# The key's norm in a stick-breaking attention: applied to the keys, or to the logits when they are evicted

## Chip, core and metric

One core of a Trainium2 chip runs the whole program. The metric is the device time of one execution in microseconds.

## What is computed

A two-layer decoder trunk over 1024 tokens of width 1024: a gated DeltaNet layer with its feed-forward part, then a cross layer whose eight heads (128 wide) attend by stick-breaking over keys and values computed once. The part that matters here, cut from the reference:

```python
def rms_norm(x, gain):
    y = x * lax.rsqrt(jnp.mean(x * x, axis=-1, keepdims=True) + EPS)
    return y * gain

k = rms_norm(k.reshape(b_, s_, SB_HEADS, SB_DH), k_gain)      # per token and head
q = rms_norm((hn @ w_q).reshape(b_, s_, SB_HEADS, SB_DH), q_gain)

z = jnp.einsum('bhtd,bhsd->bhts', qb, kb) * scale             # 128 queries, all keys up to them
ls_neg = jax.nn.log_sigmoid(-z)
log_fail = jnp.where(causal, ls_neg, 0.0)
log_rest = lax.cumsum(log_fail, axis=3, reverse=True) - log_fail
att = jnp.where(causal, jnp.exp(z + ls_neg + log_rest), 0.0)
outs.append(jnp.einsum('bhts,bhsd->bhtd', att, vb))
```

The norm of a key is one number per token s, so it may multiply the key's 128 elements, or column s of the logits.

## The kernel before

Matrix products run on pairs of fp32r tiles, a rounded part `h` and the remainder `l`, as three matmuls (h.h, h.l, l.h) into one PSUM buffer. PSUM has two sets: `ups`, three buffers, for projections; `ips`, five buffers, for transposes, logits and attention times values. A buffer is given to the next user when its last reader is done. In SBUF the tag `n` has four buffers of 128x1024, shared in this stage by the copies of projections (`f` of k, q and v), the attention's output `of`, the two parts `nh`/`nl` of one row of output weights, and, at the end, rows of the residual stream.

The stage around the change is written as generators whose steps carry a cost. `sb_steps(hd)` (attention of head `hd`) and `qkv_steps(hd + 1)` (k, q and v projections of the next head) are merged in the ratio of ATT 24000 to QKV 35000; for the last head the second stream is `part(fill, BESIDE)`, the first output projections (`down_steps`, L257 to L259, whose results ScalarE copies out at L308). This gives the order in which the program is written down; a scheduler that assigns buffers and semaphores may move an instruction ahead of others on its engine when it reckons it ready, and the order on each engine is then fixed in the program.

A projection is done in two halves of 512 tokens, 24 matmuls each (L140 to L142), with head dimension on partitions and tokens along the free axis. What is done with a half at its end is its `take`; steps that come later are put on a list by `post(delay, ...)` and run when the clock of the projection stream has passed their time.

- Query: `take` copies the half to `f` (L1516) and evicts `ql`, `qh` with the gain from the projection's buffer (L1517, L1518). 3000 later, `norm` transposes `f` (L1488, four 128x128 blocks into one `ips` buffer), squares (L1493, ScalarE), sums (L1494, VectorE) and takes the power -1/2 (L1495, L1496, GpSimd). The result has queries on partitions, and is the scale `sc` of the logits' eviction.
- Key: `take` only copies (L1550). `norm` as above, then `scale` (2000 later) multiplies the transposed block, still in its PSUM buffer, by the norm back into `f` (L1538, VectorE), and `back` (3000 later) transposes `f` again (L1488) and evicts `kh` (L1545, ScalarE) and `kl` (L1546, VectorE) with the gain.
- Value: `take` copies (L1568); 3000 later `rows` transposes and evicts `vh`, `vl` (L1563, L1564).

For each block of 128 queries, `sb_logs` makes up to two logit tiles of up to 512 keys (L1590 to L1592), from each of which ScalarE takes Abs with scale (L1593) into `l` and VectorE the scaled logit into `z` (L1594); then ScalarE does Exp (L1598) and Ln (L1599) on `l`. `sb_weights`, one block later: VectorE max and add (L1607), GpSimd's causal selects (L1609), VectorE's scan (L1613) and subtraction (L1614), ScalarE's Exp (L1616). Another block later, `sb_transpose` transposes the weights (L1629) and evicts them (L1631 ScalarE, L1632 VectorE); `sb_values` multiplies by the values (L1646 to L1648), copies out (L1650) and stores the head (L1656). Weight columns come in by DMA (L112), are scaled on GpSimd (L121) and split (L103 ScalarE, L104 VectorE).

Of the kernel before, what the change touches and what calls it, by code (L numbers as in the profile page):

```python
# [12 lines left out]
AF = mybir.ActivationFunctionType  # L13
ALU = mybir.AluOpType
# [4 lines left out]
P = 128  # L19
# [4 lines left out]
def yoco_kernel(  # L24
# [22 lines left out]
    act, dve, pool, pe, sp = nc.scalar, nc.vector, nc.gpsimd, nc.tensor, nc.sync  # L47
# [10 lines left out]
    HB = S // 2  # L58
# [16 lines left out]
    def i_tile(shape=(P, 4, P)):  # L75
        return pi.tile(list(shape), F32, tag="i", name="ips")

    def n_tile(shape=(P, S)):
        return main.tile(list(shape), F32, tag="n", name="n", bufs=4)
# [4 lines left out]
    def bc(ap, n=P):  # L84
        return ap.unsqueeze(2).broadcast_to([ap.shape[0], ap.shape[1], n])


    ident = cpool.tile([P, P], F32, name="ident")
# [82 lines left out]
    def run(gen):  # L171
        for _ in gen:
            pass
# [803 lines left out]
    with tc.tile_pool(name="gdn", bufs=1) as gp:  # L977
# [50 lines left out]
        def gain_cols(i, j, n):  # L1028
            return gains[:, offs[i] + j * n : offs[i] + (j + 1) * n]
# [4 lines left out]
        g_k = gain_cols(4, 0, 1)  # L1034
# [423 lines left out]
    with tc.tile_pool(name="sba", bufs=1) as ap_:  # L1458
        tc.keep_in_program_order(act.preload_act_table_set("natural_log_exp_and_others"))

        def sb_tile(tag, nm):
            return ap_.tile([P, S], F32R, tag=tag, name=nm, bufs=4 if tag != "v" else 3)

        posts, clock = [], [0]
        POST, SCALE, BACK = 3000, 2000, 3000

        def post(delay, fn, *args):
            posts.append((clock[0] + delay, fn, args))
            posts.sort(key=lambda p: p[0])
# [15 lines left out]
        def transpose_half(f, hf):  # L1485
            tps = i_tile()
            for j in range(4):
                pe.transpose(tps[:, j, :], f[:, hf * HB + j * P : hf * HB + (j + 1) * P], ident)  # L1488
            return tps

        def row_norm(s_, tps):
            sq = main.tile([P, 4, P], F32, tag="og", name="sq")
            act.activation(sq, tps, AF.Square, scale=float(P) ** -0.5)  # L1493
            dve.tensor_reduce(s_, sq, axis=AX.X, op=ALU.add)  # L1494
            pool.tensor_scalar(s_, s_, EPS, None, op0=ALU.add)  # L1495
            pool.tensor_tensor(s_, s_, mhalf, op=ALU.pow)  # L1496

        def z_tile(tag):
            return ap_.tile([P, S], F32, tag=tag, name=tag, bufs=3 if tag == "z" else 2)

        def f_tile(hd):
            return z_tile("z") if hd == 0 else n_tile()
# [19 lines left out]
            return take  # L1522

        def k_take(hd):
            f = f_tile(hd)
            hi, lo = sb_tile("k", "kh"), sb_tile("k", "kl")
            qkv[hd, "k"] = (hi, lo)

            def norm(hf):
                tps = transpose_half(f, hf)  # L1530
                ss = ap_.tile([P, 4], F32, tag="ss", name="ss", bufs=4)
                row_norm(ss, tps)
                post(SCALE, scale, hf, tps, ss)
                return 436

            def scale(hf, tps, ss):
                fs = f[:, hf * HB : (hf + 1) * HB].rearrange("p (a b) -> p a b", b=P)
                dve.tensor_tensor(fs, tps, bc(ss), op=ALU.mult)  # L1538
                post(BACK, back, hf)
                return 1  # L1540

            def back(hf):
                hs = slice(hf * HB, (hf + 1) * HB)
                tf = transpose_half(f, hf).rearrange("p a b -> p (a b)")
                act.activation(hi[:, hs], tf, AF.Copy, scale=g_k)  # L1545
                dve.scalar_tensor_tensor(lo[:, hs], tf, g_k, hi[:, hs], op0=ALU.mult, op1=ALU.subtract)  # L1546
                return 436

            def take(hf, sl, ps):
                act.copy(f[:, sl], ps)  # L1550
                post(POST, norm, hf)

            return take
# [19 lines left out]
        qkv, zs, ats, ofs = {}, {}, {}, {}  # L1573
# [3 lines left out]

        def sb_logs(hd, tb, later):

            (qh, ql, qs), (kh, kl) = qkv[hd, "q"], qkv[hd, "k"]  # L1580
            w = (tb + 1) * P
            ts_ = slice(tb * P, (tb + 1) * P)
            z, l = z_tile("z"), z_tile("l")
            sc = qs[:, tb : tb + 1]
            next(later, None)
            for s0 in range(0, w, 512):
                n = min(512, w - s0)
                ss_ = slice(s0, s0 + n)
                zps = i_tile((P, 512))
                pe.matmul(zps[:, :n], qh[:, ts_], kh[:, ss_], start=True, stop=False)  # L1590
                pe.matmul(zps[:, :n], qh[:, ts_], kl[:, ss_], start=False, stop=False)
                pe.matmul(zps[:, :n], ql[:, ts_], kh[:, ss_], start=False, stop=True)  # L1592
                act.activation(l[:, ss_], zps[:, :n], AF.Abs, scale=sc)  # L1593
                dve.tensor_scalar(z[:, ss_], zps[:, :n], sc, None, op0=ALU.mult)  # L1594
                yield 3 * max(107, n * 0.417)
                next(later, None)
            run(later)
            act.activation(l[:, :w], l[:, :w], AF.Exp, scale=-1.0)  # L1598
            act.activation(l[:, :w], l[:, :w], AF.Ln, bias=1.0)  # L1599
            chains[hd, tb] = (z, l)  # L1600
# [57 lines left out]
        def sb_order():  # L1658

            blocks = [(hd, tb) for hd in range(H) for tb in range(NT)]  # L1660
            n = len(blocks)
            for k in range(n + 3):
                at_ = blocks[min(k, n - 1)][0]
                later = sb_weights(*blocks[k - 1]) if 1 <= k < n + 1 else iter(())
                yield at_, sb_logs(*blocks[k], later) if k < n else later
                if 2 <= k < n + 2:
                    yield at_, sb_transpose(*blocks[k - 2])
                if k >= 3 and blocks[k - 3][1] % 2:
                    hd, tb = blocks[k - 3]
                    yield at_, sb_values(hd, tb // 2)  # L1670
# [14 lines left out]
        def head_all(hd):  # L1685
            takes = [k_take, q_take, v_take]
            if hd == 0:
                yield from proj_two_steps(norm1, [(la1.ready.pop(0), takes.pop(0)(hd)) for _ in range(2)])
                la1.fill(2)
            for take in takes:  # L1690
                last = hd == H - 1 and take is takes[-1]
                for i, cost in enumerate(proj_steps(xT, la1.get(), take(hd))):
                    yield cost
                    if last and i in (1, KT + 1):
                        next(fill)
# [92 lines left out]
```

## Time and profile before

| | us |
|---|---|
| median of 3 runs (2637.34 to 2642.93) | 2642.91 |
| the profiled execution | 2642.97 |
| its span | 2641.3 |
| TensorE busy | 2540.1 (96%) |
| VectorE busy | 1829.7 (69%) |
| ScalarE busy | 1144.9 (43%) |
| GpSimd busy | 863.8 (33%) |

The stage of the change fills about 1405 to 1910 us of the span. TensorE's busy time has the modelled ends of pipelined matmuls in it: neighbours overlap, so that gaps between them show a little smaller than they are. An instruction's row in the timeline gives start, duration, engine, line, and in brackets how long the engine stood idle before it and what released it.

### The profile page before, as it was taken

What the parts mean: (1) busy time and instruction counts of PE and PEld (TensorE: products, weight loads), DVE (VectorE), ACT (ScalarE), POOL (GpSimd) and SP (SyncE); (2) the same over time, 40 slices, a digit from 0 to 9 for tenths busy, and PEclk for the clock granted to TensorE, in tenths of its full rate; (3) what the DMA queues carried; (4) which work ended last, traced back from release to release, by engine and by line L of the source; (5) the groups of instructions that cost most, each with busy time, mean ns of one, the idle gap of its engine ahead of it and who ended that gap; (6) DMA issues with size and microseconds to landing.
All of it is one profiled execution on the core that took longest, in us unless ns stands there. A gap on an engine that the chain in (4) does not pass through costs nothing.

```text
span 2641.3 us, 35798 instructions
## 1 busy us (share of the span) xinstructions
PE 2540.1 (96%) x12908; PEld 2068.3 (78%) x12908; DVE 1829.7 (69%) x2705; ACT 1144.9 (43%) x2219; POOL 863.8 (33%) x1262
## 2 busy tenths in 40 slices
PE   8999999999999999998999999999999999999999
PEld 6777877887768888886777778887777888887777
DVE  6667766775686666667755778877658566666774
ACT  6333333334363444432215667667646444443220
POOL 2444444444411222254313243333240212225420
PEclk9999999999999999999999999999999999999999
DMA  4221222223324554578661111111333455548765
GB/s 125 63 58 54 65 54 65 69 72 100 132 65 143 170 145 134 165 248 296 230 221 66 39 34 33 32 41 63 105 128 88 122 158 168 144 136 288 272 224 203
DMA packets 368953, 331.25 MB, mean 125 GB/s; under 512 B 19572, under 2 KB 321791, under 8 KB 368775
## 3 DMA queue, kind: packets, MB, share of 16 engines
q1 hardware_dynamic: 368774, 328.96, 39.9%
q8 instruction: 101, 1.65, 0.3%
q14 instruction: 78, 0.63, 0.1%
HBM read 226.10 MB, written 102.79 MB: 125 GB/s over the span
## 4 chain that ended last, share of the span: by engine, by line
PE 58%; DVE 14%; issue 12%; POOL 5%; ACT 5%; DMA 4%; SPq 0%; POOLq 0%; DVEq 0%; ACTq 0%
PE ips L453 6%; PE ips L454 6%; PE ips L455 6%; PE ups L140 5%; PE ups L454 4%; PE ups L455 4%; PE ups L453 4%; PE ups L141 4%; PE ups L142 4%; DVE l L1613 2%; PE ips L1143 2%; DVE wl L104 2%; PE ups L258 2%; PE ups L259 2%; PE ups L257 2%
## 5 line engine op out<-in xcount | busy, mean ns | idle before, releaser
L140 PE MATMUL ups<-x,wh 128*128 128x512 f32 (+1 forms) x912 | 388.7, 427 | 0.0
L142 PE MATMUL ups<-x,wl 128*128 128x512 f32 (+1 forms) x912 | 363.1, 399 | 0.0
L141 PE MATMUL ups<-x,wh 128*128 128x512 f32 (+1 forms) x912 | 359.4, 394 | 0.0
L453 PE MATMUL ips<-x,w 128*128 128x512 f32 x840 | 328.5, 393 | 7.3 <-ACT x L359 3.7
L454 PE MATMUL ips<-x,w 128*128 128x512 f32 x840 | 328.7, 391 | 2.7 <-DVE x L360 2.7
L455 PE MATMUL ips<-x,w 128*128 128x512 f32 x840 | 327.5, 390 | 0.0
L552 POOL TENSOR_TENSOR n<-n,ev 128x512 f32<-128x512 f32 x44 | 70.2, 1596 | 627.4 <-ACT n L551 627.4
L453 PE MATMUL ups<-x,w 128*128 128x512 f32 x648 | 252.0, 392 | 2.0 <-ACT x L359 2.0
L454 PE MATMUL ups<-x,w 128*128 128x512 f32 x648 | 253.5, 391 | 0.3 <-DVE x L360 0.3
L455 PE MATMUL ups<-x,w 128*128 128x512 f32 x648 | 252.7, 390 | 0.0
L142 PEld LDWEIGHTS ups<-x,wl 128*128 128x128 f32 (+1 forms) x912 | 170.8, 187 | 37.4
L453 PEld LDWEIGHTS ips<-x,w 128*128 128x128 f32 x840 | 157.6, 188 | 46.6 <-ACT x L359 6.3
L140 PEld LDWEIGHTS ups<-x,wh 128*128 128x128 f32 (+1 forms) x912 | 171.9, 189 | 22.6 <-ACT x L231 0.2
L141 PEld LDWEIGHTS ups<-x,wh 128*128 128x128 f32 (+1 forms) x912 | 172.2, 189 | 21.4 <-DVE x L232 0.2
L454 PEld LDWEIGHTS ips<-x,w 128*128 128x128 f32 x840 | 158.0, 188 | 39.0 <-DVE x L360 5.8
L455 PEld LDWEIGHTS ips<-x,w 128*128 128x128 f32 x840 | 157.9, 188 | 32.7
L746 DVE TENSOR_TENSOR h<-h,ips 128x512 f32<-128x512 f32 x176 | 119.4, 682 | 61.5 <-PE ips L455 61.3
L453 PEld LDWEIGHTS ups<-x,w 128*128 128x128 f32 x648 | 121.5, 188 | 28.9 <-ACT x L359 3.6
L454 PEld LDWEIGHTS ups<-x,w 128*128 128x128 f32 x648 | 121.9, 188 | 26.8 <-DVE x L360 1.6
L455 PEld LDWEIGHTS ups<-x,w 128*128 128x128 f32 x648 | 121.9, 188 | 24.9
L746 DVE TENSOR_TENSOR h<-h,ups 128x512 f32<-128x512 f32 x136 | 92.5, 682 | 47.0 <-PE ups L455 46.7
L104 DVE TENSOR_TENSOR wl<-raw,wh 128x1024 fp32r<-128x1024 f32 x65 | 83.5, 1284 | 53.9 <-ACT wh L103 51.4
(377 smaller groups left out, 5983.4 us busy)
## 6 DMA issues: line engine op xcount, KB each, us to landing
raw<-in_ffn_w_gu_dram SPq DMA_DIRECT2D x88, 512.0 KB, 4.8
w<-hsa SPq DMA_DIRECT2D x88, 512.0 KB, 4.6
hsa<-w SPq DMA_DIRECT2D x116, 256.0 KB, 3.1
hb<-hsb SPq DMA_DIRECT2D x68, 384.0 KB, 4.2
raw<-in_ffn_w_down_dram SPq DMA_DIRECT2D x44, 512.0 KB, 4.3
raw<-in_gdn_w_in_dram SPq DMA_DIRECT2D x32, 512.0 KB, 4.2
hsb<-w SPq DMA_DIRECT2D x54, 256.0 KB, 3.6
hsa<-n SPq DMA_DIRECT2D x48, 256.0 KB, 3.6
```

Source lines behind the costliest of these rows:

```text
L104: dve.tensor_tensor(lo, raw, hi, op=ALU.subtract)
L140: pe.matmul(o, wh[:, kt, :m], xh, start=kt == 0, stop=False)
L141: pe.matmul(o, wh[:, kt, :m], xl, start=False, stop=False)
L142: pe.matmul(o, wl[:, kt, :m], xh, start=False, stop=kt == KT - 1)
L257: pe.matmul(ps, ah[:, sl], wh[:, ns], start=i == 0, stop=False)
L258: pe.matmul(ps, ah[:, sl], wl[:, ns], start=False, stop=False)
L259: pe.matmul(ps, al[:, sl], wh[:, ns], start=False, stop=i == n - 1)
L453: pe.matmul(ps, ah, bh, start=start, stop=False, skip_group_check=True)
L454: pe.matmul(ps, ah, bl, start=False, stop=False, skip_group_check=True)
L455: pe.matmul(ps, al, bh, start=False, stop=stop, skip_group_check=True)
L552: pool.tensor_tensor(s, s, self.t3, op=ALU.mult)
L746: dve.tensor_tensor(d, d, ps, op=ALU.add)
```

## The change

The keys are no longer scaled. `kh` and `kl` are evicted in `take`, unscaled by the norm, from the projection's buffer, as the query's are. `norm` computes the four columns of a half (128 tokens on partitions, 4 blocks). `scale` and `back` are gone; 6000 after `norm`, `spread` transposes each column, repeated 128 times along the free axis, which gives 128 equal rows with tokens along the free axis, and ScalarE copies the four blocks to `rk`: 128x1024, the key's norm of each token on all partitions. `rk` is the key's own `f` (for head 0 a new `n` tile) and lives until the logits of its head are done. The logits' eviction multiplies by `sc` and by `rk` on VectorE; Abs then reads `z` from SBUF instead of the logits from PSUM.

```diff
-        POST, SCALE, BACK = 3000, 2000, 3000
+        POST, SPREAD = 3000, 6000
...
         def k_take(hd):
+
+            hi, lo = sb_tile("k", "kh"), sb_tile("k", "kl")
             f = f_tile(hd)
-            hi, lo = sb_tile("k", "kh"), sb_tile("k", "kl")
-            qkv[hd, "k"] = (hi, lo)
+            rk = [None if hd == 0 else f]
+            qkv[hd, "k"] = (hi, lo, rk)
 
             def norm(hf):
-                tps = transpose_half(f, hf)
                 ss = ap_.tile([P, 4], F32, tag="ss", name="ss", bufs=4)
-                row_norm(ss, tps)
-                post(SCALE, scale, hf, tps, ss)
+                row_norm(ss, transpose_half(f, hf))
+                post(SPREAD, spread, hf, ss)
                 return 436
 
-            def scale(hf, tps, ss):
-                fs = f[:, hf * HB : (hf + 1) * HB].rearrange("p (a b) -> p a b", b=P)
-                dve.tensor_tensor(fs, tps, bc(ss), op=ALU.mult)
-                post(BACK, back, hf)
-                return 1
-
-            def back(hf):
-                hs = slice(hf * HB, (hf + 1) * HB)
-                tf = transpose_half(f, hf).rearrange("p a b -> p (a b)")
-                act.activation(hi[:, hs], tf, AF.Copy, scale=g_k)
-                dve.scalar_tensor_tensor(lo[:, hs], tf, g_k, hi[:, hs], op0=ALU.mult, op1=ALU.subtract)
+            def spread(hf, ss):
+                if rk[0] is None:
+                    rk[0] = n_tile()
+                bps = i_tile()
+                for j in range(4):
+                    pe.transpose(bps[:, j, :], ss[:, j : j + 1].broadcast_to([P, P]), ident)
+                act.copy(rk[0][:, hf * HB : (hf + 1) * HB], bps.rearrange("p a b -> p (a b)"))
                 return 436
 
             def take(hf, sl, ps):
                 act.copy(f[:, sl], ps)
+                act.activation(hi[:, sl], ps, AF.Copy, scale=g_k)
+                dve.scalar_tensor_tensor(lo[:, sl], ps, g_k, hi[:, sl], op0=ALU.mult, op1=ALU.subtract)
                 post(POST, norm, hf)
...
-            (qh, ql, qs), (kh, kl) = qkv[hd, "q"], qkv[hd, "k"]
+            (qh, ql, qs), (kh, kl, (rk,)) = qkv[hd, "q"], qkv[hd, "k"]
...
-                act.activation(l[:, ss_], zps[:, :n], AF.Abs, scale=sc)
-                dve.tensor_scalar(z[:, ss_], zps[:, :n], sc, None, op0=ALU.mult)
+                dve.scalar_tensor_tensor(z[:, ss_], zps[:, :n], sc, rk[:, ss_], op0=ALU.mult, op1=ALU.mult)
+                act.activation(l[:, ss_], z[:, ss_], AF.Abs)
```

## Rows read from the trace of the kernel before

**Rows 1.** The page, engines: busy us (share of the span) x instructions.
```profile
PE 2540.1 (96%) x12908; PEld 2068.3 (78%) x12908; DVE 1829.7 (69%) x2705; ACT 1144.9 (43%) x2219; POOL 863.8 (33%) x1262
```

**Rows 2.** Windows: length, busy us per engine (instructions), granted clock, DMA share, GB/s.
```profile
1440.00:1840.00 400.00, 380.18 (x2099) 320.37 (x2098) 318.60 (x440) 269.06 (x495) 142.43 (x236) 1.00 0.12 38
1840.00:1910.00 70.00, 61.57 (x316) 50.99 (x315) 43.62 (x61) 46.02 (x85) 18.55 (x24) 0.95 0.34 112
```

**Rows 3.** TensorE's waits, 1440 to 1840: us in total, times, longest.
```profile
PE ips L1488 <- DVE z L1594: 7.5, 10, 2.2
PE ips L1590 <- DVE kl L1546: 6.3, 6, 1.2
PE ips L1629 <- ACT z L1616: 2.5, 4, 0.9
PE ips L1488 <- DVE n L1538: 1.6, 1, 1.6
```

**Rows 4.** Timeline around a wait for `kl`: start, us, engine, line, operation, [idle before].
```profile
1578.09 0.62 PE L1488 MATMUL ips<-ident,n 128*128 128x128 f32 x4
...
1578.77 0.58 ACT L1493 ACTIVATE sq<-ips 128x512 f32<-128x512 f32 x1
...
1582.77 0.72 DVE L1546 SCALAR_TENSOR_TENSOR kl<-ips,gains,kh 128x512 fp32r<-128x512 f32 x1
...
1583.54 0.50 PE L1590 MATMUL ips<-kh,qh 128*128 128x512 f32 x1 [1.23 <-DVE kl L1546]
...
1583.88 0.39 PE L1591 MATMUL ips<-kl,qh 128*128 128x512 f32 x1
...
1584.11 0.40 PE L1592 MATMUL ips<-kh,ql 128*128 128x512 f32 x1
...
1585.20 0.68 DVE L1538 TENSOR_TENSOR n<-ips,ss 128x512 f32<-128x512 f32 x1
```

**Rows 5.** Timeline at the boundary of two heads.
```profile
1610.54 1.06 ACT L1616 ACTIVATE z<-z 128x1024 f32<-128x1024 f32 x1 [4.93 <-DVE z L1614]
...
1613.71 0.34 DVE L1594 TENSOR_SCALAR z<-ips,ssq 128x128 f32<-128x128 f32 x1
...
1614.11 0.65 PE L1488 MATMUL ips<-ident,n 128*128 128x128 f32 x4 [1.42 <-DVE z L1594]
```

**Rows 6.** Groups by form, 1400 to 1915: count | busy us, mean ns | idle before.
```profile
L1594 DVE TENSOR_SCALAR z<-ips,ssq 128x512 f32<-128x512 f32 x48 | 35.7, 743 | 4.4 <-ACT l L1593 4.4
L1593 ACT ACTIVATE l<-ips,ssq 128x512 f32<-128x512 f32 x48 | 33.0, 688 | 6.2 <-PE ips L1592 6.0
...
L1488 PEld LDWEIGHTS ips<-ident,n 128*128 128x128 f32 x232 | 26.4, 141 | 16.0 <-DVE z L1594 9.6 <-ACT n L1568 2.1 <-issue 2.0
...
L1538 DVE TENSOR_TENSOR n<-ips,ss 128x512 f32<-128x512 f32 x14 | 9.6, 684 | 9.6 <-POOL ss L1496 9.6
...
L1598 ACT ACTIVATE l<-l 128x512 f32<-128x512 f32 x8 | 5.2, 644 | 0.0
```

**Rows 7.** Timeline at the end of head 6, and line L308, 1840 to 1900.
```profile
1829.20 0.74 DVE L1594 TENSOR_SCALAR z<-ips,ssq 128x512 f32<-128x512 f32 x1
...
1830.31 0.60 PE L1488 MATMUL ips<-ident,n 128*128 128x128 f32 x4
...
1831.66 1.21 DVE L104 TENSOR_TENSOR nl<-raw,nh 128x1024 fp32r<-128x1024 f32 x1
...
1833.80 0.61 ACT L1568 COPY n<-ups 128x512 f32<-128x512 f32 x1
...
1842.19 0.66 PE L1488 MATMUL ips<-ident,n 128*128 128x128 f32 x4 [1.48 <-ACT n L1568]
...
1870.05 0.32 SPq L1656 DMA_DIRECT2D oT<-n  x1
...
L308 ACT COPY x<-ups x16: 567/587/635, 1849.5 to 1895.9; 128x512 f32<-128x512 f32 x16
```

**Rows 8.** Timeline, the last transposes that waited for the exponential before 1840.
```profile
1461.09 0.66 PE L1629 MATMUL ips<-ident,z 128*128 128x128 f32 x4 [0.85 <-ACT z L1616]
```

## Prediction

> **What bounds the kernel now.** The page's engine shares come first: TensorE is busy 96% of the span [rows 1], so time is gained only where TensorE stands still or runs slowly. The change touches one stage, the stick-breaking attention, so next I read the windows of that stage. From 1440 to 1840 us, while the attention of heads 0 to 6 runs beside the projections of heads 1 to 7, TensorE is busy 380.18 of 400 us, VectorE 318.60, ScalarE 269.06; from 1840 to 1910, head 7 beside the first output projection, TensorE has 61.57 of 70 us and a granted clock of 0.95 [rows 2]. What can be won in the first window is thus 19.8 us of visible gaps, plus some 0.16 us a gap (a 512-column matmul is drawn 0.39 long but the next starts 0.23 after it [rows 4]). Then TensorE's waits: the largest are transposes waiting for the logits' eviction on L1594 (7.5 us), the first logit matmul waiting for `kl` on L1546 (6.3 us), attention transposes waiting for the exponential L1616 (2.5 us), and one wait of 1.6 us for the key scaling L1538 [rows 3]. None of the first two is a data dependence: the transposes don't read `z`, and that matmul reads an older head's keys. They wait for a PSUM buffer: `ips` has five, and all transposes, logits and values take turns in them.
>
> The timeline around one such wait shows why. The norm's transposes of a key half start at 1578.09; their square has read them by 1579.35, yet the buffer is held until L1538 has read it too, at 1585.88, because that instruction waits for the GpSimd power. The buffer of the way back is held until L1546 ends at 1583.49, and TensorE's matmul starts at 1583.54, after 1.23 us of nothing [rows 4]. This wait comes five times at 1.23 us and once at 0.15 (6.3 us in six) [rows 3].
>
> **The change part by part.**
> 1. *L1538 goes.* Sixteen halves, 0.684 us each [rows 6]: 10.9 us of VectorE, which isn't the bound. Its worth is the buffer: the norm's is now free after the square (0.58 us [rows 4]) instead of 6.5 us later.
> 2. *`kh` and `kl` are made at the take, from the projection's own PSUM buffer `ups`*, as the query does it. L1545/L1546 move (0.72 us for the latter [rows 4]), at no cost. They hold `ups` longer; there are three, a projection half takes 24 matmuls at 0.23 = 5.5 us, and that covers it. Without the cover, each half would cost the 0.7 us of one eviction. The way back's hold of `ips` until L1546 is gone.
> 3. *`spread` is added*: four transposes replace the four of the way back, one for one, and one ScalarE copy of 128x512 per half: as the output projection's copy of the same shape, 0.587 [rows 7], 16 of them 9.4 us, beside TensorE. It is due 9000 cost units after the take where the way back was due 8000; `rk` is read a head later, so the 1000 cost nothing. ScalarE is busy 67% in the window [rows 2] and hides it; uncovered on the way to the buffer it costs 0.6 a half. The copy frees its `ips` buffer; it stands where `kl` stood but doesn't wait behind VectorE's scans. The stationary operand is one column read 128 times, which no row shows. The nearest row is the ordinary fp32 weight load at 0.141 us [rows 6]; I take that. Bounds: half and double of it, 64 loads x 0.07, from -4.5 to +4.5 us when none is hidden by a running matmul (as an estimate from that row).
> 4. *The logits' eviction.* Before, ScalarE's Abs reads the buffer (0.688 us), then VectorE (0.743) [rows 6], one after the other. Now VectorE alone reads it, with `rk` as second tensor: the nearest row with a PSUM input and a second SBUF tensor is L1546 at 0.72 [rows 4], so at par with 0.743. The Abs then reads `z` from SBUF; nearest row, the SBUF-to-SBUF L1598 at 0.644 against 0.688 [rows 6]: 48 x 0.044 = 2 us less on ScalarE. So each logit buffer can be free some 0.7 us earlier, and VectorE needn't wait for ScalarE to free it. The price is latency: z, Abs, Exp, Ln now stand in one row where Abs came first and z ran beside Exp, +0.70 us per block; and Abs now sits in ScalarE's queue until VectorE has done z, with the takes' copies and the attention casts behind it.
>  [...]
> 5. *`rk` lives in an `n` buffer* (four of them, shared by the takes' copies, the attention's output `of`, and two weight tiles `nh`, `nl`) until the last logits of its head. Between heads this just fits. At the end of head 6 it doesn't: `rk` of head 6 is read until 1829.9 (L1594), `rk` of head 7 and `of` of head 6 stay (its last store is issued at 1870.05), the query's copy until its transposes at 1830.31. `nh` and `nl` (now at 1831.66) take the two that come free, and the value's copy, now at 1833.80, finds none until `of` is stored [rows 7]. Two of three `ups` buffers stay full, and the output projection beside it runs on one: each of its steps waits for its own copy. Sixteen copies run from 1849.5 to 1895.9, one per 3.1 us [rows 7]; in the 28 us from 1842 to 1870 that is nine steps x 0.587 = 5.3 us at most, less what attention work fills. Lower bound 0 (head 7's attention moves up instead and frees `of` early). If the value's copy gets its buffer first, `nl` waits for the transposes at 1842.19 [rows 7], 2 to 3 us late. I take 3 us.
>
> *Sum, against the profiled execution (span 2641.3, time 2642.97, as good as the median 2642.91).*
> - `kl` waits gone: 5 x (1.23 + 0.16) + 0.3 = 7.3 us, all.
> - L1538's wait gone: 1.6 + 0.16 = 1.8.
> - The waits on L1594: ten, 7.5 us, the longest 2.2 [rows 3]; the long ones lie at the head boundaries. There ScalarE stands 4.93 us for the last block's L1614, the weight cast and VectorE's L104 behind it come late, and the 128-column z is only evicted at 1613.71, whereupon the transposes start at 1614.11 [rows 5]. With z no longer behind Abs it may go before L104, and it may not, since the order on VectorE is set when the kernel is built. Half: 0.5 x (7.5 + 10 x 0.16) = 4.6.
> - Against it: head 0's four waits for L1616 (2.5 us in four [rows 3], at the stage's start, where blocks are short) grow by up to 0.70 each; half, 1.4. Tail: 3.
>
> 7.3 + 1.8 + 4.6 - 1.4 - 3.0 = 9.3 us gained: 2642.97 - 9.3, about **2634 us**. Next late behind the removed waits are the attention transposes behind `attl` and L1616.
>
> **The rivals.**
> - *Gaps come back.* With `ips` free earlier TensorE runs into the next buffer or into L1616, whose own chain VectorE's scans set; VectorE is 80% busy [rows 2]. For it: VectorE loses only 3% of its work. Against: the five 1.23 us waits have two buffers of five returned, not one. Half of the `kl` gain and none of the boundary's remain: 3.7 + 1.8 + 1 - 1.4 - 3 = 2 us, **2641**.
> - *The longer row sets the end (slower).* Place: ScalarE's queue at Abs. If ScalarE, waiting for z behind a scan, delays casts by more than TensorE's reserve of other matmuls, each block pays the 0.70 us. It decides from the point where L1616 is waited for in steady state; today the last of its four waits ends at 1461.09 [rows 8]. At 64 blocks x 0.70 = 45 us in full; at half of heads 0 and 7 and a fifth of the others (8 + 48 x 0.2 = 18 blocks, 12 us) against 2 us of gain left: **2653**. [...]
> - *The `n` buffers bite harder (slower).* If the store of `of` or `nl` comes so late that the output projection stops altogether from 1842 to 1870, nine steps x 9 matmuls x 0.23 = 18.6 us move out of cover; half is refilled later by the attention: -12.3 of gain + 9.3, **2640**, and in full **2649**.
> - *It doesn't do what it says*: the transposes of a repeated column cost double (+4.5) and the freed buffers are hidden anyway: **2645**.
>
> **How the numbers follow.** Forecast (2626 to 2638) 0.56; gaps come back 0.22; longer row 0.10; buffers 0.08 (half of it on each side of the bound); not as said 0.04. The low end takes all listed waits (7.3 + 1.8 + 9.1), no tail cost and half of the transposes' bound (2.2): 20.4 us, 2622. The high end reaches to 2650, short of the full longer row. The bound of 0.2% is 5.3 us (about what a measurement of this kernel can tell from no change): below 2637.6 faster, above 2648.2 slower. Faster: the forecast and a little of the second case, 0.58; same 0.27; slower 0.15.
>
> **What would show it.** Right: no wait of L1590 for the keys' eviction; the norm's transposes freed by the square; ScalarE's Abs released by VectorE's z, VectorE's z by TensorE; TensorE idle from 1440 to 1840 down from 19.8 to some 8 us; the value's copy of head 7 late, near the last store of `of`, and the steps of L257 slowed there. Wrong: waits of L1629 for L1616 in heads 1 to 6, weight loads of the spread above 0.19 us, or a window to 1910 longer than 470 us.

## The result, and the profile after

The changed kernel is slower: 2675.31 us, the median of four runs (2671.61 to 2677.34), against 2642.66 for the kernel before on the same chip. The ratio is 1.0122, with a 95% interval of 1.011 to 1.0134; in time 32 us lost, where 9 us gained were forecast. The profiled execution took 2677.34 us, its span is 2675.4.

The page of the changed kernel, engines (busy us, share of the span, instructions), to be held against [rows 1]:

```profile
PE 2550.8 (95%) x12908; PEld 2066.1 (77%) x12908; DVE 1828.2 (68%) x2689; ACT 1147.8 (43%) x2235; POOL 867.6 (32%) x1262
```

TensorE has the same number of instructions, and no other engine's busy time moved by more than 4 us. Of the 34 us of span TensorE's busy time has 10.7, and the rest is TensorE standing still. The windows of the changed kernel say where (columns as in [rows 2]):

```profile
1440.00:1840.00 400.00, 376.93 (x2083) 315.98 (x2082) 305.06 (x417) 264.12 (x498) 138.71 (x232) 1.00 0.11 35
1840.00:1910.00 70.00, 49.16 (x175) 33.03 (x173) 17.01 (x18) 25.54 (x42) 11.55 (x9) 0.85 0.22 68
...
1860.00:1880.00 20.00, 16.02 (x48) 11.09 (x49) 1.23 (x1) 3.48 (x7) 0.00 (x0) 0.77 0.19 54
```

Against [rows 2] there are two losses of different kinds. While heads 0 to 6 run, TensorE does 2083 matmuls in 400 us instead of 2099: a small, steady loss. From 1840 to 1910 it does 175 instead of 316, at a granted clock of 0.85 instead of 0.95, and VectorE and ScalarE have next to nothing to do (1.23 and 3.48 of 20 us, from 1860 to 1880): something has stopped the attention altogether.

TensorE's waits in the changed kernel, 1400 to 1945 (us in total, times, longest), to be read against [rows 3]:

```profile
PE ups L257 <- ACT x L308: 11.5, 15, 2.1
PE ips L1628 <- ACT z L1615: 10.8, 12, 2.1
PE ips L1488 <- ACT n L1567: 10.1, 9, 1.8
PE ups L257 <- ACT kh L103: 6.0, 1, 6.0
PE ups L259 <- DVE x L1714: 2.8, 2, 1.8
PE ips L1542 <- DVE attl L1631: 2.5, 6, 0.5
```

Behind the keys' part lines are one lower than before: L1628 is the transposition of the weights, L1615 their Exp, L1567 the value's copy. `z` is L1592, Abs L1593; L1542 is new, the spread. The two waits that the change was to remove, for `kl` and for L1538, are gone. Three others took their place (L1628, L1488 for the value's copy, L1542), and the output projection waits for its own copies.

The forms of the moved and added work, same stretch (count | busy us, mean ns | idle before):

```profile
L1592 DVE SCALAR_TENSOR_TENSOR z<-ips,ssq,n 128x512 f32<-128x512 f32 x48 | 35.5, 741 | 1.5 <-PE ips L1591 1.5
L1593 ACT ACTIVATE l<-z 128x512 f32<-128x512 f32 x48 | 30.1, 630 | 32.1 <-DVE z L1592 32.0
L1543 ACT COPY n<-ips 128x512 f32<-128x512 f32 x16 | 9.4, 588 | 3.7 <-PE ips L1542 3.7
L1542 PEld LDWEIGHTS ips<-ident,ss 128*128 128x128 f32 x64 | 7.2, 136 | 6.5 <-DVE attl L1631 5.1 <-POOL ss L1496 0.3
```

Every duration came out as costed: 741 ns for the eviction with a second tensor (743 before), 588 for the spread's copy (0.587 taken), 136 for a repeated column as weights (0.141 taken). What was missed is not the length of any instruction. The idle time of Abs is new: 32.0 us of waiting for `z`, where it had 6.2 us, nearly all for TensorE [rows 6].

Of the end, the timeline of the changed kernel, ScalarE, TensorE and VectorE (start, us, engine, line, [idle before]):

```profile
1837.26 0.75 DVE L1592 SCALAR_TENSOR_TENSOR z<-ips,ssq,n 128x512 f32<-128x512 f32 x1
...
1839.15 0.94 ACT L1615 ACTIVATE z<-z 128x896 f32<-128x896 f32 x1
...
1842.61 1.06 ACT L103 CAST nh<-raw 128x1024 fp32r<-128x1024 f32 x1
...
1856.05 0.79 PE L257 MATMUL ups<-kh,x 128*128 128x512 f32 x1 [6.03 <-ACT kh L103]
...
1875.62 0.59 ACT L308 COPY x<-ups 128x512 f32<-128x512 f32 x1 [2.44 <-PE ups L259]
1878.65 0.59 ACT L308 COPY x<-ups 128x512 f32<-128x512 f32 x1 [2.44 <-PE ups L259]
...
1908.27 1.06 ACT L1567 COPY n<-ups 128x512 f32<-128x512 f32 x2
1908.89 0.66 PE L1488 MATMUL ips<-ident,n 128*128 128x128 f32 x4
...
1909.98 0.31 PE L1589 MATMUL ips<-kh,qh 128*128 128x128 f32 x1
1910.35 0.95 PE L1628 MATMUL ips<-ident,z 128*128 128x128 f32 x7
```

The last logits of head 6 are evicted at 1838.01, and block 6 of that head has its Exp at 1840.09, ready to be transposed. The transposes (L1628) start at 1910.35, seventy microseconds later. In between the sixteen steps of the output projection run one behind the other, 3.03 us apart from the third on, each waiting for the copy of the last. From 1845 to 1908 TensorE runs nothing but these steps (L257 to L259). The value's copy, at 1833.80 in the kernel before [rows 7], is at 1908.27, behind fifteen of those sixteen copies; 0.6 us later everything starts again at once.

A measure for both losses is the distance between the first logit matmuls (query block 0) of neighbouring heads, read from the timelines, in us (the profile of before has a granted clock of 0.64 from 1730 to 1732 and 0.51 from 1732 to 1734, by an estimate from these some 1.7 us of its distance of 60.2):

| | heads 0 to 7, distances | last logits |
|---|---|---|
| before | 52.7 56.2 57.7 57.8 57.7 60.2 59.4 | 1905.2 |
| after | 53.5 58.1 58.8 58.7 58.9 58.8 **119.8** | 1939.1 |

About 1 us a head in the steady part, and 60 us before head 7, a part of which the output projection, run ahead, gives back.

### The profile page after: what moved, and what is told of

It reads as the page before. It is cut to its first block, busy times and chain, and to the rows that moved or that the text cites. A ratio compares the mean times of both kernels' runs of the same rounds, so it can differ in the third digit from the quotient of the medians.

```text
span 2675.4 us, 35802 instructions
## 1 busy us (share of the span) xinstructions
PE 2550.8 (95%) x12908; PEld 2066.1 (77%) x12908; DVE 1828.2 (68%) x2689; ACT 1147.8 (43%) x2235; POOL 867.6 (32%) x1262
## 4 chain that ended last, share of the span: by engine, by line
PE 61%; DVE 14%; issue 9%; POOL 6%; ACT 5%; DMA 4%; SPq 0%; POOLq 0%; DVEq 0%; ACTq 0%
PE ips L453 7%; PE ips L454 7%; PE ips L455 7%; PE ups L454 5%; PE ups L455 5%; PE ups L453 5%; PE ups L140 5%; PE ups L141 4%; PE ups L142 4%; DVE l L1612 2%; PE ips L1143 2%; PE ups L257 2%; PE ups L259 2%; PE ups L258 2%; DMA raw<-in_w_kv_dram 1%
```

## The experiments

Each ratio is to runs of the kernel before that were made beside it on the same chip (four groups, with medians of 2640.28, 2640.51, 2641.24 and 2641.41 us). Distances are those of the heads, as above.

**The end alone, mended.** The first output weights, `nh` and `nl` among them, are loaded behind the first half of head 7's value projection instead of at its second step, so that they take no `n` buffer ahead of the value's copy:

```diff
-                    if last and i in (1, KT + 1):
+                    if last and i in (KT, KT + 1):
```

> The changed kernel with one thing moved: the loads and splits of the first output weights (nh, nl among them) begin after the first half of head 7's value projection instead of at its second step, so that the value's copy asks for its n buffer before they do. Buffer theory (the n buffers cost the changed kernel its tail): the attention of head 7 runs beside the output projection again, the stretch from 1840 us on loses some 28 us, 2645 to 2650 in all. Rival (the tail is slow because of the new eviction's longer row, the buffers only coincide): 2668 to 2675.

Measured: 2649.92 us, ratio 1.0039 (1.0026 to 1.0052). The last distance is 61.0 instead of 119.8, the last logits stand at 1913.5. Two thirds of the loss were in this place; the steady heads are as slow as in the changed kernel (58.6).

**The end alone, made.** The kernel before, with nothing but a longer hold of the key's `n` buffer, by a 128x1 product that reads `f` after the last logits of the head:

```diff
+            held[hd] = f
...
+                if s0 + n == S and hd > 0:
+                    dve.tensor_tensor(seen, z[:, S - 1 : S], held[hd][:, S - 1 : S], op=ALU.mult)
```

> The kernel before, with the key's copy f held in its n buffer until the last logits of its head are evicted (a 128x1 VectorE product of z and f that nobody uses, once per head 1 to 7, some 0.1 us each); keys and eviction as before. Buffer theory: the tail of the changed kernel appears in it, sixteen steps of the output projection at 3.0 us one by one, head 7's attention after them: 2668 to 2675. Rival (the loss needs the new eviction): 2643 to 2646.

Measured: 2667.86, ratio 1.01 (1.0078 to 1.0122). Heads at 57.7, as before, and the last distance 117.5. The hold costs 26 us by itself (0.01 x 2640), without spread, without a new eviction. The waits of its end are those of the changed kernel (L257 for L308 11.7 us in 15 and L257 for `kh` 6.3).

**The eviction alone.** The kernel before with `z` first and Abs from `z`, keys scaled as they were:

```diff
-                act.activation(l[:, ss_], zps[:, :n], AF.Abs, scale=sc)
                 dve.tensor_scalar(z[:, ss_], zps[:, :n], sc, None, op0=ALU.mult)
+                act.activation(l[:, ss_], z[:, ss_], AF.Abs)
```

> The kernel before with the eviction's order alone changed: VectorE takes z from PSUM first, ScalarE's Abs reads z from SBUF; keys normalised as before. Theory of the steady stretch (ScalarE waits at Abs for VectorE, and what is queued behind it comes late): a head takes some 58.8 us in place of 57.7, 2648 to 2653. Rival (logit buffers come free earlier, and the slower heads of the changed kernel come from the eviction of kh and kl at the take): at most 2643.

Measured: 2643.34, ratio 1.0009 (0.9999 to 1.0019), heads 57.6 to 57.7, one of them 58.4. The longer row of z, Abs, Exp, Ln and the logits' buffer freed earlier come together to nothing that can be measured; the run doesn't separate the two. The waits for `kl` grew to 11.3 us in six, and the transposes' waits for the logits' eviction went.

**The keys' part alone.** The changed kernel with the logits evicted as before; the norm is spread but multiplied nowhere:

> The changed kernel with the logits evicted as before; the key's norm is computed and spread but multiplied nowhere, so that rk is free as soon as it is written. Theory of the steady stretch: without the new eviction the waits for kl are gone and nothing takes their place, a head takes 56 to 57 us, 2632 to 2638. Rival (the take's burst slows the heads): a head takes 58 us or more, 2646 or more.

Measured: 2658.69, ratio 1.0072 (1.0054 to 1.0091), heads 61.4 to 61.5: slower still than the whole change. Both expectations named a direction, and neither its cause. The timeline of this kernel, GpSimd, VectorE and TensorE:

```profile
1517.44 3.99 POOL L121 TENSOR_TENSOR raw<-raw,gains 128x256 f32<-128x256 f32 x4 [0.33 <-DMA raw<-in_w_kv_dram]
...
1522.84 0.29 POOL L1608 TENSOR_SCALAR_AFFINE_SELECT l<-l 128x128 f32<-128x128 f32 x1
...
1523.16 1.55 DVE L1612 TENSOR_TENSOR_SCAN l<-l 128x640 f32<-128x640 f32 x1 [2.21 <-POOL l L1608]
...
1526.91 0.66 PE L1628 MATMUL ips<-ident,z 128*128 128x128 f32 x4 [1.53 <-ACT z L1615]
...
1529.24 0.58 PE L1645 MATMUL ips<-atth,vh 128*128 128x256 f32 x1 [0.86 <-DVE attl L1631]
...
1532.21 1.11 PE L1488 MATMUL ips<-ident,n 128*128 128x128 f32 x4 [1.53 <-DVE z L1593]
```

At the bottom are three waits of TensorE: for the Exp, for the eviction of the transposed weights (L1631) and for that of the logits. From there upwards: the Exp is late for a scan that waited 2.21 us; the scan for GpSimd's causal select; the select stands behind 3.99 us of weight scaling (L121), and the norm's two steps after it, in GpSimd's queue. This theory is tested below.

**The steps at the take, put off.** The first run above (end mended), with `kh` and `kl` evicted at the spread, from `f` in SBUF, instead of at the take:

> The kernel of e1_fill_later with kh and kl evicted at the spread, from the copy f in SBUF, just ahead of the copy of rk, instead of at the take from PSUM; the take copies only, as in the kernel before. Theory of the take (three evictions on ScalarE at the end of a key half delay what follows): heads at 57.7 us or less, 2640 to 2645. Rivals (place of the spread; GpSimd): 58.6 us a head, 2648 to 2652.

Measured: 2649.36, ratio 1.0031 (1.0021 to 1.0041), heads 58.6, one of them 59.1. Nothing moved: it makes no difference that these two evictions stand at the take.

**The spread 1000 earlier.** End mended, and

```diff
-        POST, SPREAD = 3000, 6000
+        POST, SPREAD = 3000, 5000
```

> The kernel of e1_fill_later with the spread due 5000 after the norm instead of 6000, so at 8000 after the take, where the way back was due before. Theory of the place (the spread's four transposes and copy fall where they collide): heads back to 57.7 us, 2640 to 2645. Rivals (the eviction at the take; GpSimd): 58.6 us a head as before, 2648 to 2652.

Measured: 2640.77, ratio 1.000 (0.999 to 1.001), heads 56.9 to 57.7. A step of four transposes and one copy, moved by 1000 cost units (by an estimate some 1.9 us: the projections of a head, 57.7 us long, are 48 steps of 642), is worth 9 us (2649.92 less 2640.77). It doesn't move alone: on all four engines other instructions change places with it (Abs against Exp and Ln, logits against values, selects), so the 9 us are those of the new order as a whole. TensorE's waits from 1500 to 1800, first with the spread at 6000 (end mended), then at 5000:

```profile
PE ips L1488 <- ACT n L1567: 10.2, 9, 1.8
PE ips L1628 <- ACT z L1615: 4.8, 5, 1.1
PE ips L1542 <- DVE attl L1631: 2.2, 5, 0.5
```

```profile
PE ips L1488 <- ACT n L1516: 4.7, 5, 1.0
PE ips L1628 <- ACT z L1615: 4.3, 5, 1.1
PE ips L1589 <- DVE attl L1631: 2.0, 5, 0.4
```

**The same place, tried on the kernel before.** `BACK` 4000 instead of 3000, so that the old way back falls due where the changed kernel had its spread:

> The kernel before with BACK 4000 in place of 3000, so that the way back of the key falls due 9000 after the take, as the spread did in the changed kernel. Theory 'any step of that place, a transposition and an eviction, is worse at 9000 than at 8000': 2645 to 2652 against 2640.5. Theory 'only the spread is, since there its copy stands in ScalarE's queue behind Abs': 2638 to 2643.

Measured: 2648.61, ratio 1.0028 (1.0018 to 1.0038), heads 59.1. So the delay isn't harmless without the spread either: the kernel before loses 7 us by the same 1000. It loses them by another wait than the changed kernel did. The waits for `kl` are gone, and the largest from 1400 to 1945 is a new one, of the logits for a buffer that L1538 holds:

```profile
PE ips L1590 <- DVE n L1538: 13.7, 6, 2.5
```

That wait again has GpSimd's queue at its root, by the timeline of this kernel: weight scaling from 1578.47 to 1581.80, then two selects, then the norm's addition (1.28 us) and power, and L1538 only at 1584.81.

**GpSimd's weight scaling left out.** The kernel before without the multiplication of the weights by the gain of the input's norm (L121) for the projections of this stage, which changes the output:

```diff
-        src = {"q": (sb_w_q[0], 0, g_attn[1]), "k": (w_kv, 0, g_kv), "v": (w_kv, H, g_kv)}
+        src = {"q": (sb_w_q[0], 0, None), "k": (w_kv, 0, None), "v": (w_kv, H, None)}
```

> The kernel before without GpSimd's multiplication of the q, k and v weights by the layers' gains in this stage (left out). GpSimd theory (the middle gap of each head comes from the causal selects queued behind that multiplication, which hold up VectorE's scan and all behind it): the 1.23 us wait for kl and the head boundary's wait go without any change of the keys, heads of 56 to 56.5 us, 2630 to 2635. Rival (the buffers of the keys' way back hold TensorE by themselves): 57.5 us a head, 2640 to 2643.

Measured: 2628.41, ratio 0.9948 (0.9933 to 0.9963), heads 54.8. Its waits of TensorE from 1500 to 1800 (in the kernel before, 7.3 and 6.1 us in this stretch):

```profile
PE ips L1488 <- DVE z L1594: 1.2, 5, 0.2
PE ips L1590 <- DVE kl L1546: 0.2, 1, 0.2
```

Nothing of the keys' buffers was changed in this kernel, and the waits for them are gone. VectorE's waits of the scan for the select from 1500 to 1800, in the kernel before and in this one:

```profile
DVE l L1613 <- POOL l L1609: 18.2, 20, 2.7
```

```profile
DVE l L1613 <- POOL l L1609: 3.7, 11, 0.5
```

L121 apart, the two traces have the same instructions in the same order on TensorE, VectorE, ScalarE and GpSimd from 1400 to 1830, so a new order isn't what gained the 12 us. In the round of [rows 4] the scaling takes GpSimd from 1577.75 to 1581.01, the select follows at 1580.97, the scan at 1581.29 after 1.23 us of waiting, and `kl` stands behind the scan on VectorE at 1582.77. TensorE's 1.23 us of waiting at 1583.54 are that wait, handed on.

**The changed kernel without it.** End mended, spread at 6000, no weight scaling:

> The kernel of e1_fill_later without the same multiplication. GpSimd theory: its waits for the exponential in the middle of a head go as well, heads at most 57 us, 2636 to 2641, and so near e10 that the change is worth nothing or costs up to 5 us even then. Rival (the change's own chain through z and Abs on ScalarE sets the heads): 58 us a head or more, 2645 to 2650.

Measured: 2635.65, ratio 0.9977 (0.9967 to 0.9986), heads 56.7. It is 7 us above the kernel before with the same omission: GpSimd isn't all of it. TensorE's waits of this kernel, 1500 to 1800, and the head boundary on ScalarE and TensorE:

```profile
PE ips L1488 <- ACT n L1567: 8.7, 5, 1.8
PE ips L1542 <- DVE attl L1631: 1.5, 5, 0.3
```

```profile
1596.20 0.63 ACT L1593 ACTIVATE l<-z 128x512 f32<-128x512 f32 x1 [2.74 <-DVE z L1592]
1596.74 0.67 ACT L1517 ACTIVATE qh<-ups,g_q 128x512 fp32r<-128x512 f32 x1
1597.31 0.94 ACT L1615 ACTIVATE z<-z 128x896 f32<-128x896 f32 x1
...
1600.77 0.61 ACT L1493 ACTIVATE sq<-ips 128x512 f32<-128x512 f32 x1
1601.26 0.60 ACT L1567 COPY n<-ups 128x512 f32<-128x512 f32 x1
...
1601.91 0.66 PE L1488 MATMUL ips<-ident,n 128*128 128x128 f32 x4 [1.75 <-ACT n L1567]
```

ScalarE stands 2.74 us at Abs for `z`, which is behind the scan on VectorE; then a full queue is worked off, and the value's copy comes at its end. TensorE wants to transpose that copy and waits 1.75 us, once a head. With the spread at 5000 this wait isn't there, though Abs still waits for `z` (26.4 us in all, 128x512 tiles); in the eviction run, which has the same Abs but no spread, it isn't either (2.1 us in two, from 1400 to 1945).

**The scaling moved instead of left out.** First by due times: the four multiplications of a unit 1200 cost units apart, in the kernel before and in the changed one (end mended, spread at 5000). In both the value's weights are read at other columns than they should be, which changes the output and not the work.

> The kernel before, with one move: the four GpSimd multiplications (L121) that scale a projection's weights, so far in one row as soon as the weights have landed, are put on the list of later steps one by one, 1200 cost units apart, and the split into wh and wl follows behind the last. Nothing is left out. Theory 'GpSimd's row of four ahead of the causal selects makes the waits': heads fall from 57.7 towards the 54.8 us that they took without these multiplications, six times 1.5 to 3 us, so 2624 to 2633 against 2640.5. Rival 'it is the amount of GpSimd work, wherever it stands': 2637 to 2641. A second rival, that the later split makes the projections wait for their weights: above 2645, with TensorE waiting for wh or wl.

> The changed kernel with the output weights' loads after head 7's first value half and the spread at 5000 (2640.8 in its run), and the GpSimd multiplications one by one as in the run beside it. If the changed kernel's freed buffers are worth something once GpSimd no longer holds up the selects, it is 3 us or more below the kernel before with the same move. If they were only another way round GpSimd's row, the two are within 2 us of each other, both 2624 to 2633. If the changed row of z, Abs, Exp and Ln costs by itself, it is 3 to 8 us above it.

Measured: 2638.76, ratio 0.999 (0.9981 to 0.9998), and 2644.34, ratio 1.0009 (1.0001 to 1.0018). This tells little: GpSimd's timeline of the first shows that the multiplications were put back in a row ahead of a select when the program's order was made:

```profile
1520.93 3.06 POOL L1683 TENSOR_TENSOR raw<-raw,gains 128x256 f32<-128x256 f32 x4 [1.77 <-DMA raw<-in_w_kv_dram]
1523.94 0.29 POOL L1609 TENSOR_SCALAR_AFFINE_SELECT l<-l 128x128 f32<-128x128 f32 x1
```

So it was bound by data: for q and v units of heads 2 to 7 the multiplications read a copy of the gain made from the last scan, and can't start ahead of it.

```diff
+            g = ap_.tile([P, KT], F32, tag="gl", name="gl", bufs=2)
+            dve.scalar_tensor_tensor(g, l[:, :KT], 0.0, gain, op0=ALU.mult, op1=ALU.add)
...
+                pool.tensor_tensor(raw[:, ks], raw[:, ks], bc(g[:, ks]), op=ALU.mult)
```

> The kernel before; nothing is left out. For the q and v units of heads 2 to 7 the four GpSimd multiplications read the gain from a small copy that VectorE makes out of the running block's scan (gain + 0 x l), so they can only start behind a scan, when the next selects are a block away; the k unit's stay as they were. Theory 'it is the row's place ahead of the selects': the waits for kl lose most of their 1.23 us, heads 55 to 57 us instead of 57.7, 2627 to 2637 against 2641. Rival 'it is the amount of GpSimd work': 2639 to 2644. If the later split makes projections wait for wl: above 2645, with waits of L142 or L141 for it.

> The same edit on the changed kernel with the spread at 5000 and the output weights' loads after head 7's first value half (2640.8 without the edit). If place is the cause and the freed buffers are only another way round it: within 3 us of the run beside it. If the freed buffers are worth something of their own: 3 us or more below it. If the row of z, Abs, Exp and Ln costs of its own: 3 to 8 us above it.

Measured: 2643.79, ratio 1.0008 (0.9999 to 1.0017), and with the change 2666.6, ratio 1.0089 (1.0076 to 1.0103), heads 61.6. By the total, the theory of the place failed (2627 to 2637 expected), and the number is in the range of its rival, the amount of work. By the waits it is the other way: those for `kl` fell to 2.0 us in six. But the heads gain hardly anything, with 57.0 to 57.1 us for heads 1 to 3 and 58.3 to 58.4 for the next two: transposes of the weights now wait for the copy of attention times values, and the value's copy of head 7 is late. TensorE's waits of that kernel, 1400 to 1945:

```profile
PE ips L1631 <- ACT n L1652: 10.7, 6, 1.8
PE ips L1488 <- ACT n L1568: 5.4, 1, 5.4
...
PE ips L1590 <- DVE kl L1546: 2.0, 6, 0.3
```

The total is not better, and for the changed kernel it is far worse. Its largest wait is then one of the weights' transposes for the square of a norm (L1493), 11.1 us in six; why, was not followed further. That a better place for this work exists is thus not shown; only that leaving it out gives 12 us.

**The norm spread onto the keys.** A form without the longer hold: norm, spread 5000 later, VectorE multiplies `f` by the spread norm and the gain in place, `kh` and `kl` follow from SBUF; logits evicted as before.

```diff
+                dve.scalar_tensor_tensor(f[:, hs], bf, g_k, f[:, hs], op0=ALU.mult, op1=ALU.mult)
+                act.copy(hi[:, hs], f[:, hs])
+                dve.tensor_tensor(lo[:, hs], f[:, hs], hi[:, hs], op=ALU.subtract)
```

> The kernel before with the key's norm still multiplied into the keys, but by way of the spread: the norm's transposes are free after the square, L1538 and the second transposition of the key go, the four columns are spread by transposes of repeated columns 5000 after the norm, VectorE multiplies f by them and by the gain in place, ScalarE rounds kh and VectorE takes kl from SBUF. Logits are evicted as before, no n buffer is held longer. Theory 'the gain lies in the norm's buffer freed early, and the eviction and the longer life of rk are not needed for it': 2632 to 2640 against 2640.5. Theory 'the waits are set by GpSimd and only move': 2638 to 2644. If the three dependent steps at the end hold the buffer as L1546 did: up to 2648.

Measured: 2648.07, ratio 1.0028 (1.0016 to 1.004), heads 57.6 to 60.4. L1538 and the way back are gone here as well, and the transposes wait 16.2 us in six for the logits' eviction instead. No run that computes the whole reference was faster than the kernel before.

## Why the prediction was wrong, and where it was right

**Tail, point 5: "I take 3 us".** The mechanism was right in its first half: the value's copy, in the forecast's words, "finds none", and the steps of L257 are slowed. It was wrong on what ends this: not the store of `of`, which is issued only at 1920.59, after the copy at 1908.27. The size was wrong by nearly ten times: 22 us by the difference of the two ratios (1.0122 and 1.0039), 26 us when made alone in the kernel before. The step that failed is the bound "nine steps x 0.587 = 5.3 us at most, less what attention work fills", and with it the end "0 (head 7's attention moves up instead and frees `of` early)". Attention filled nothing: from 1845 to 1908 TensorE runs only L257 to L259. The transposes of the value's rows are written down before head 7's logits and before the last transposes of head 6, and buffers of `ips` go to their users in that order: while the first of these waits for the value's copy, nobody behind it gets one. The weights of head 6, ready at 1840.09, aren't transposed until 1910.35, so `of` isn't complete, so no `n` buffer comes free from there; only the end of the output projection, with `nh` and `nl`, breaks the ring. The row is the gap between L1615 and L1628 in the timeline above; that it is order and not a data dependence is read from the program and from TensorE's rows of this gap, and no run takes the order itself apart. That the `n` hold sets it off is shown by both runs. The rival on the `n` buffers asked the right question, whether "the output projection stops altogether", but it was the attention that stopped.

**Spread, point 3: "the 1000 cost nothing".** It costs 9 to 10 us (1.0039 against 1.000 of 2640). The reason given was that `rk` is read a head later. That is true of the result. But the step's own instructions take places in TensorE's and ScalarE's queues and a turn in `ips`, and these move others: at 6000 TensorE waits for the value's copy once or twice a head (10.2 us in nine), at 5000 it doesn't. Which instructions have to stand next to each other for that was not settled, and other instructions than the spread's changed places too. The kernel before loses by the same delay of its way back (1.0028), but by waits for L1538, so that it is one place that costs in both is not shown.

**The sum: 7.3 + 1.8 + 4.6.** The waits for `kl` and L1538 went, and the gain didn't come. This is the rival "gaps come back", and the reason in it, that VectorE's scans set L1616, is half of the matter. For five kernels, the waits that the view of TensorE lists from 1500 to 1800, divided by the heads in these 300 us:

| | waits, us a head | heads, us | difference |
|---|---|---|---|
| before | 13.4 / 5.2 = 2.6 | 57.7 | 55.1 |
| after, end mended | 17.2 / 5.1 = 3.4 | 58.6 | 55.2 |
| the same, spread at 5000 | 11.0 / 5.25 = 2.1 | 57.1 | 55.0 |
| before, no weight scaling | 1.4 / 5.5 = 0.3 | 54.8 | 54.5 |
| after, end mended, no weight scaling | 10.2 / 5.3 = 1.9 | 56.7 | 54.8 |

In these five a head is 55 us of TensorE and its waits. (In the run with the keys' part alone it is 61.5 less 20.6 / 4.9 = 4.2, or 57.3; there the granted clock was 0.94 from 1500 to 1800 as well.) The forecast took the waits for [rows 3] as the price of a held buffer. By the run without weight scaling, in which the order is the same, they were the price of a late chain, that of GpSimd, scan, Exp, which showed up at whatever buffer came next: free that buffer, and the same lateness is waited for at the transposition of the weights. In the changed kernel at 1590.98 TensorE waits 1.13 us for L1615, and in front of it GpSimd's scaling runs from 1582.46 to 1585.24, the norm's two steps and the select follow at 1587.10, the scan at 1587.43. The forecast followed [rows 4] back to L1538 and "the GpSimd power" and stopped one step short of what the power and the selects stood behind.

The three steps account for the miss: some 19 us more at the tail than the 3 taken, 9 to 10 for the spread's place, and 12 us (7.3 + 1.8 + 4.6 - 1.4) that moved instead of going, since with the end mended and the spread at 5000 the kernel is at par. That makes the 41 us between 9 us gained and 32 lost.

**The longer row (rival).** Net of the buffer freed earlier it costs nothing (1.0009, with 0.9999 to 1.0019), so the price of 0.70 us a block doesn't show. The place may have been right: ScalarE stands at Abs for 32 us in the changed kernel, and in the rows of the run without scaling the value's copy is late behind such a stop (1.75 us a head). But with the spread at 5000 it stands there for 26.4 us and the copy is in time, so the stop alone doesn't make it late.

**What came out as forecast.** Durations of all moved and added operations; the takes' evictions at no cost (1.0039 with them at the take, 1.0031 with them put off); the load of the repeated column (136 ns against 141 for a block of `n`, inside the bounds of half and double, of which the upper one should have been 64 x 0.141 = 9.0 us and not 4.5); Abs released by `z`, `z` by TensorE. Abs came out at 630 ns from SBUF against 688 from PSUM, as the row had it. But the two forms differ in more than the memory: the one from PSUM took its scale from a tensor. ScalarE's evictions of 128x512 from PSUM with such a scale take 680 to 697 ns in the two kernels (L1517, L1545), and its forms from PSUM without one 571 to 590 (copies, L1516, L1543 and L308) and 596 (the square, L1493). So by these rows what Abs gained goes with the scale, and against forms without one the row from SBUF is 34 to 59 ns longer; no run has Abs itself in both places with the same scale. The forecast's own signs of being wrong, waits for the Exp in heads 1 to 6 and a window to 1910 that isn't enough, are both in the profile; and TensorE's idle time from 1440 to 1840, which was to fall from 19.8 to some 8 us, rose to 23.1.

What stays open: whether the change could gain anything in an order made for it. With the end mended and the spread at 5000 it is at par (0.999 to 1.001), and one shift of other work made that 1.0089.

## What to carry to other kernels

Before costing a wait for a buffer at what frees it, follow the chain of the late instruction back through every engine's queue until something stands there that waits for nothing; here a buffer freed short of that only moved the wait (TensorE's waits were 2.6 us a head before, 3.4 with the change and its end mended). When a change lengthens the hold of a shared buffer, look for the first user that then finds none and ask what is written down behind it in every other pool it takes from: here the ring of waits cost 22 to 26 us, where 5.3 was taken as the most. And where an order is fixed when the program is built, a step that "has time" still has a place (a move by 1000 cost units was worth 9 us for the spread, 7 for the old way back): try two places before judging the change.

## What the runs showed of the hardware

After short stops in mid-stream TensorE's granted clock fell in places from 1.00 to 0.50. In the run with the keys' part alone, windows around its three waits (columns as in [rows 2]):

```profile
1526.00:1529.00 3.00, 1.46 (x8) 1.02 (x8) 1.86 (x4) 2.88 (x5) 0.34 (x2) 0.98 0.02 5
1529.00:1532.00 3.00, 1.43 (x5) 1.14 (x5) 3.00 (x4) 2.97 (x6) 0.20 (x1) 0.50 0.00 0
1532.00:1534.00 2.00, 1.79 (x7) 1.70 (x8) 2.00 (x4) 1.61 (x4) 0.00 (x0) 0.50 0.00 0
1534.00:1536.00 2.00, 2.00 (x9) 1.80 (x9) 2.00 (x5) 0.43 (x2) 0.51 (x2) 0.58 0.00 0
1536.00:1538.00 2.00, 2.00 (x12) 1.66 (x11) 1.91 (x1) 0.94 (x3) 1.85 (x2) 1.00 0.00 0
```

TensorE had been busy 1.46 of 3 us when the clock fell, and was back at 1.00 after some 6 us. In the run with `BACK` 4000 one wait of 2.45 us did the same: 512-column matmuls start 0.42 us apart after it (1586.53, 1586.96, 1587.38) instead of 0.23, until about 1589.5 (granted clock 0.53 from 1586 to 1588, 0.61 from 1588 to 1590). That wait cost more than its length: by an estimate from these starts some 3.5 us at half speed, 1.8 us beside the 2.45. Not every such wait did: of that run's five waits of 2.45 to 2.46 us from 1500 to 1800, those ending at 1585.55 and 1762.96 were followed by starts 0.42 us apart, the other three by starts 0.23 us apart. With the norm spread onto the keys four of five waits of 2.79 to 2.80 us were followed by starts 0.42 to 0.43 us apart, and the wait of 2.18 us in the kernel before that ends at 1730.30 by a granted clock of 0.51 from 1732 to 1734. The waits of 1.0 to 1.8 us in the changed kernel left no such mark (granted clock 1.00 from 1500 to 1800). The forecast had priced a wait by its length and 0.16 us; where the clock fell to 0.50 behind a wait, it cost more.
